# A two-layer retention and state-space decoder: the opening's norm ranked first, and the SSD norm's weight loaded earlier

## The chip, the cores and the metric

The kernel runs on one core of one Trainium2 chip. The metric is device time of one execution in microseconds (us); a kernel's time is the median over its runs. The engines are TensorE (PE), VectorE (DVE), ScalarE (ACT), GpSimd (POOL) and SyncE (SP), which only issues DMAs here. Each engine executes its instructions in the order of the program and waits on semaphores where an input isn't there yet.

## The reference

What is computed, cut to its frame (sequence 256, width 1024, two layers, float32):

```python
def hybrid_mixer(h, ...):                       # h is rmsnorm(x, norm_mix_w[l])
    u = h @ w_in
    q, k, v, g_ret, z, xbc, dt, gate_ret, gate_ssd = split(u)
    qf, kf = rotary(q, pos), rotary(k, pos) * RET_DK ** -0.5
    yr = retention(qf, kf, v)                   # 4 heads, decaying causal attention in chunks of 128
    yr = silu(g_ret) * (yr * rsqrt(mean(yr * yr) + EPS))
    o_ret = yr @ ret_out
    xs, bm, cm = split(silu(causal_dwconv(xbc, conv_w, conv_b)))
    ys = ssd_scan(xs * dtp, dtp * a, bm, cm) + d_skip * xs      # 32 heads in 4 groups
    ys = ys * silu(z)
    ys = ys * rsqrt(mean(ys * ys, per group) + EPS) * ssd_norm_w
    o_ssd = ys @ ssd_out
    return (sigmoid(gate_ret) * o_ret + sigmoid(gate_ssd) * o_ssd) @ w_o

for l in range(DEPTH):
    h = h + hybrid_mixer(rmsnorm(h, norm_mix_w[l]), ...)
    h = h + swiglu(rmsnorm(h, norm_ffn_w[l]), w_gate_up[l], w_down[l])
return rmsnorm(h, final_norm_w)
```

## The kernel before

All activations stay in SBUF; the weights, some 260 MB with what is read more than once, stream in from HBM. The 256 tokens are two halves of 128 (`t` is 0 or 1). Each float32 product is made of three float32r matmuls: a weight piece (`raw`, up to 128x1024 elements, 512 KB) arrives by DMA, ScalarE copies its high part (`wh`, L506), VectorE subtracts to get the low part (`wl`, L531), and TensorE multiplies high by high, low by high and high by low (L548, L549 and L550 with the weights stationary, L1034 and L1037 with the activations `xT` stationary). Some projections use a seven-product scheme on sums of weight blocks, which VectorE forms (L230) or a DMA issued by POOL adds up while it loads (L413).

**The order of the work** is set when the program is built, by a planner (`Flow`). Streams (Python generators) yield operations, each with an engine, an estimated cost, an emitting function and a priority `pr`; an engine of the planner's model takes the ready operation with the smallest `pr`, the older one on a tie. What each engine takes, in that order, is the program. The chip then follows that order, whatever its own durations are. Jobs (one projection each) have priorities from 0 up, in their order; the splitting of a job's weights stands a little ahead of the job. A `yield` on a slot semaphore such as `wbS` waits until a buffer is free.

**Weight loads** go through SyncE's queue (`feeder`, L486), in the order of the jobs, each as a `raw` slot comes free. Other loads are put in between: `BESIDE` (L206) gives for each entry of the list `others` (L2229) the number of the weight piece ahead of which it goes. The list holds the four quarters of x for the norm (`O`), constants, the opening norm's weight (the sixth entry), parameters, constants, and the starts of two tables (`tables(0)` is `load_angles`, `tables(1)` `load_decays`).

**The opening.** The first products (two heads of v, L874, `C` holding split x) are made from x before it is normed, twelve matmuls for each of eight k blocks; then comes the first job of the retention gate (`gr`, 48 matmuls of width 352, L548 to L550). Beside them the opening norm is worked out for each token half: ScalarE squares and sums x (`sil,ss<-O`), VectorE makes the mean (`ms`), POOL the power (`rstd`, L243), VectorE scales by `rstd` and the weight `wb` (`sil<-O,rstd,wb`, L233, two instructions of 512 columns), TensorE transposes (`tr<-cst,sil`, L644, eight of 128x128 for a half), ScalarE copies the high part into `xT`, VectorE subtracts the low part (`xT<-tr,xT`), and ScalarE keeps a plain copy (`plain`). `arrived` (L2185) starts this with the priority `PR0` (L205, 1.2). The jobs after gr use `xT`, the first with L1034.

**The buffer `wb`** (512 KB, one slot, `wbS`) holds by turns: the opening norm's weight, the rotary angles (`load_angles`, L1573, its DMA at L1580), the two halves of the SSD norm's weight (`ssd_w(0)`, `ssd_w(1)`), the FFN norm's weight, the next layer's norm weight. `load_wb` (L667) waits for the slot, issues a broadcast DMA (L672) from POOL, or from SyncE for the opening, and waits for its landing. The angles give up the slot after their last use in `rotary` (`turned` at 0, L1484). Both `ssd_w` streams are started when the job z begins in the plan (`z_begins`, L1892). Their loads are first used by z's norm (`sil<-sil,rz,wb`).

**The retention output stage** (layer 0 around 303 to 330 us, layer 1 around 922 to 948 us) multiplies the retention output by sums of the blocks of `ret_out` and `w_rw`: SyncE loads `raw<-in_w_rw_dram` and `raw<-in_ret_out_dram`, POOL issues accumulating loads `raw` and `dec<-in_w_rw_dram` (L413), ScalarE copies finished accumulators out of PSUM (`sx<-acc`, L223) between its weight copies, and TensorE's next group of matmuls into that accumulator (L548) waits for the copy. SyncE also loads `seg<-acs` there for the SSD scan.

Of the kernel before, what the change touches and what calls it, by code (L numbers as in the profile page):

```python
# [192 lines left out]
def trunk_kernel(  # L193
# [8 lines left out]
    SLOW, MT_SLACK = 1500.0, 800.0  # L202
    ADDS = 600.0
    ZS_PR, SAVE, DEC_AT = 1.0, 2000.0, 9000.0
    PR0, SLACK = 1.2, 2500.0  # L205
    BESIDE = (9, 11, 13, 15, 10, 14, 15, 15, 46, 44)  # L206
    APARTS, SUMS_PR = {}, 3.5
    cp = ctx.enter_context(tc.tile_pool(name="cp", bufs=1))
    wp = ctx.enter_context(tc.tile_pool(name="wp", bufs=HB))
# [7 lines left out]
    fl = Flow()  # L217
# [257 lines left out]
    def feeder(beside):  # L475

        for i, (src, k, n, job, (sem, alloc), land) in enumerate(specs):
            for at, gen in beside:
                if at == i:
                    yield from gen  # L480
            yield sem
            queue, eng, pr = (nc.sync, "sp", job) if i else (nc.scalar, "act", -4)

            def load():
                raw = alloc()
                queue.dma_start(out=raw[:, : k * n], in_=src)  # L486
                return raw

            raw = yield Op(eng, 450, load, pr)
            fl.spawn(land(raw, fl.transfer(512 * k * n, 4 * k * n)))  # L490
# [176 lines left out]
    def load_wb(src, pr, eng="pool"):  # L667
        yield wbS

        def emit():  # L670
            w = new_wb()
            (nc.sync if eng == "sp" else nc.gpsimd).dma_start(out=w, in_=src.partition_broadcast(P))  # L672
            return w

        w = yield Op(eng, 450 if eng == "sp" else 1050, emit, pr)
        yield fl.transfer(4 * P * D)
        return w
# [633 lines left out]
    def layer(l, mix, nxt, opening=None):  # L1311
# [261 lines left out]
        def load_angles():  # L1573
            if l:
                yield DEC_AT
            yield wbS

            def emit():
                w = new_wb()
                nc.sync.dma_start(out=w[:, : 2 * SEQ], in_=consts[:, K_COS:K_DEC])  # L1580
                return w[:, :SEQ], w[:, SEQ : 2 * SEQ]

            a = yield Op("sp", 450, emit, -1)
            fl.transfer(8 * P * SEQ)
            fl.set(angles, a)

        if l:
            fl.spawn(load_decays())
            fl.spawn(load_angles())
        else:  # L1590
            first_tables.extend([load_angles, load_decays])
# [271 lines left out]
        def ssd_w(i):  # L1863
            w = yield from load_wb(ssd_norm_w[l][i * D : (i + 1) * D], at_job[0])
            fl.set(wbs[i], w)
# [25 lines left out]

        def z_begins(g):  # L1892
            if g == 0:
                for i in range(2):
                    fl.spawn(ssd_w(i))
            if g == 2:
                fl.spawn(seven_sums(zops, yz, (0, 1), "A", at_job[0] + ZS_PR))

        def z_job(g):
            z_begins(g)  # L1900
            return tm_job(xT, z_post(g))
# [266 lines left out]
    def whole():  # L2168
# [62 lines left out]
        fl.spawn(opening.load(0))  # L2231
        fl.spawn(feeder([*zip((2, 6, 7), (opening.load(i) for i in range(1, 4))), *zip(BESIDE, others)]))
        for l in range(DEPTH):
            yield from layer(l, norms[l], norms[l + 1], None if l else opening)
# [87 lines left out]
```

## Time and profile before

| what | value |
|---|---|
| median of 3 runs | 1253.92 us (1253.69 to 1253.99) |
| the profiled execution's own time | 1253.99 us |
| its span in the profile | 1252.2 us |
| TensorE busy | 1238.6 us, 99% |
| VectorE, ScalarE, POOL busy | 1104.9 us (88%), 872.7 us (70%), 72.7 us (6%) |
| mean granted TensorE clock | 0.999 |
| bytes moved, mean rate | 266.07 MB, 212 GB/s |

How to read it: the span runs from the first to the last instruction of the trace; the execution's own time holds about 1.8 us more around it. In a timeline row stand the start, the duration, the engine, the line, the operation, the tile written and the tiles read, and in brackets how long the engine stood idle just before and what ended that. Matmuls overlap, so their durations are longer than their spacing; a loss on TensorE is read from the starts. `SPq` rows are DMA issues.

### The profile page before, as it was taken

What the parts mean: (1) busy time and instruction counts of PE and PEld (TensorE: products, weight loads), DVE (VectorE), ACT (ScalarE), POOL (GpSimd) and SP (SyncE); (2) the same over time, 40 slices, a digit from 0 to 9 for tenths busy, and PEclk for the clock granted to TensorE, in tenths of its full rate; (3) what the DMA queues carried; (4) which work ended last, traced back from release to release, by engine and by line L of the source; (5) the groups of instructions that cost most, each with busy time, mean ns of one, the idle gap of its engine ahead of it and who ended that gap; (6) DMA issues with size and microseconds to landing.
All of it is one profiled execution on the core that took longest, in us unless ns stands there. A gap on an engine that the chain in (4) does not pass through costs nothing.

```text
span 1252.2 us, 17656 instructions
## 1 busy us (share of the span) xinstructions
PE 1238.6 (99%) x6293; PEld 1052.0 (84%) x6293; DVE 1104.9 (88%) x1515; ACT 872.7 (70%) x1310; POOL 72.7 (6%) x92
## 2 busy tenths in 40 slices
PE   9999999999999999999999999999999999999997
PEld 7889888888788788888888898888888888888886
DVE  6998888889899978999798978879889998899995
ACT  7967776886766565786586676867957664776863
POOL 0000000001012001001000000000010110010000
PEclk9999999999999999999999999999999999999999
DMA  9658455566777757877776574554676776678871
GB/s 349 234 147 287 149 188 183 166 212 148 259 247 186 236 184 232 300 214 221 242 259 228 141 247 163 174 181 152 235 203 217 237 217 219 218 207 255 295 208 62
DMA packets 76343, 266.07 MB, mean 212 GB/s; under 512 B 8768, under 2 KB 9664, under 8 KB 76256
## 3 DMA queue, kind: packets, MB, share of 16 engines
q1 hardware_dynamic: 68272, 236.93, 54.2%
q0 software_dynamic: 7552, 27.38, 12.0%
q8 instruction: 49, 0.80, 0.3%
q10 hardware_dynamic: 432, 0.66, 0.2%
q14 instruction: 38, 0.31, 0.1%
HBM read 262.76 MB, written 2.16 MB: 212 GB/s over the span
## 4 chain that ended last, share of the span: by engine, by line
PE 69%; issue 2%; DVE 1%; DMA 1%; ACT 1%; POOLq 0%; POOL 0%; DVEq 0%; ACTq 0%
PE acc L548 15%; PE acc L550 15%; PE acc L549 15%; PE acc L1034 12%; PE acc L1037 6%; PE tr L644 2%; DMA raws<-in_w_sw_dram 1%; PE yps L1784 1%; DVE wl L531 1%; ACT wh L506 1%; DVE D L230 0%; PE ips L1771 0%; DVE sx L230 0%; PE tr L1671 0%; PE acc L1500 0%
## 5 line engine op out<-in xcount | busy, mean ns | idle before, releaser
L531 DVE TENSOR_TENSOR wl<-raw,wh 128x1024 fp32r<-128x1024 f32 (+2 forms) x387 | 457.1, 1197 | 42.2 <-ACT wh L506 41.0
L506 ACT ACTIVATE wh<-raw 128x1024 fp32r<-128x1024 f32 (+2 forms) x387 | 395.2, 1037 | 118.5 <-PE acc L550 49.7
L1034 PE MATMUL acc<-xT,wh 128*128 128x512 f32 x960 | 251.0, 395 | 1.0 <-DVE xT L230 1.0
L548 PE MATMUL acc<-wh,xT 128*128 128x512 f32 (+1 forms) x568 | 220.6, 388 | 0.0
L550 PE MATMUL acc<-wh,xT 128*128 128x512 f32 (+1 forms) x568 | 216.1, 380 | 0.0
L549 PE MATMUL acc<-wl,xT 128*128 128x512 f32 (+1 forms) x568 | 215.9, 380 | 0.0
L1034 PEld LDWEIGHTS acc<-xT,wh 128*128 128x128 f32 x960 | 170.3, 189 | 29.6 <-DVE xT L230 1.3
L1037 PEld LDWEIGHTS acc<-xT,wl 128*128 128x128 f32 x960 | 131.8, 190 | 9.9
L1037 PE MATMUL acc<-xT,wl 128*128 128x256 f32 x960 | 136.2, 283 | 0.0
L549 PEld LDWEIGHTS acc<-wl,xT 128*128 128x128 f32 x568 | 106.7, 188 | 20.8 <-issue 1.4
L548 PEld LDWEIGHTS acc<-wh,xT 128*128 128x128 f32 x568 | 106.7, 188 | 20.5 <-issue 1.4
L550 PEld LDWEIGHTS acc<-wh,xT 128*128 128x128 f32 x568 | 106.7, 188 | 19.6
L506 ACT ACTIVATE wh<-raws 128x1024 fp32r<-128x1024 f32 x80 | 83.9, 1057 | 46.9 <-DVE raws L230 16.5
L531 DVE TENSOR_TENSOR wl<-raws,wh 128x1024 fp32r<-128x1024 f32 x80 | 96.6, 1220 | 16.0 <-ACT wh L506 15.7
L548 PE MATMUL acc<-wh,A 128*128 128x512 f32 x224 | 88.6, 395 | 0.0
L550 PE MATMUL acc<-wh,A 128*128 128x512 f32 x224 | 87.6, 391 | 0.0
L549 PE MATMUL acc<-wl,A 128*128 128x512 f32 x224 | 87.2, 389 | 0.0
L233 DVE SCALAR_TENSOR_TENSOR cc<-cc,cv 128x255 f32<-128x255 f32 (+2 forms) x144 | 67.6, 478 | 11.4 <-ACT cc L223 10.3
L550 PEld LDWEIGHTS acc<-wh,A 128*128 128x128 f32 x224 | 42.0, 188 | 9.4 <-DVE A L230 0.5
L223 ACT ACTIVATE sx<-acc 128x512 f32<-128x512 f32 (+1 forms) x62 | 32.5, 525 | 25.0 <-PE acc L1034 14.2
L549 PEld LDWEIGHTS acc<-wl,A 128*128 128x128 f32 x224 | 42.1, 188 | 8.3
L548 PEld LDWEIGHTS acc<-wh,A 128*128 128x128 f32 x224 | 42.1, 188 | 8.4
(202 smaller groups left out, 1992.7 us busy)
## 6 DMA issues: line engine op xcount, KB each, us to landing
raw<-in_w_tm_dram SPq DMA_DIRECT2D x100, 512.0 KB, 4.1
raw<-in_w_fm_dram SPq DMA_DIRECT2D x80, 512.0 KB, 3.9
raw<-in_w_gf_dram SPq DMA_DIRECT2D x40, 512.0 KB, 4.4
raw<-in_w_gate_up_dram SPq DMA_DIRECT2D x32, 512.0 KB, 7.2
raw<-in_w_down_dram SPq DMA_DIRECT2D x28, 512.0 KB, 6.0
raw<-in_w_gr_dram SPq DMA_DIRECT2D x24, 352.0 KB, 4.3
seg<-acs SPq DMA_DIRECT2D x16, 512.0 KB, 5.9
raw<-in_ret_out_dram SPq DMA_DIRECT2D x16, 512.0 KB, 4.2
```

What stands on the lines that cost most here:

```text
L223: return Op("act", cost, lambda: nc.scalar.activation(out=out, in_=in_, func=func, **kw), pr, TABLES.get(func))
L233: return Op("dve", 1.04 * n + 130, lambda: nc.vector.scalar_tensor_tensor(out=out, in0=in0, scalar=scalar, in1=in1, op0=op0, op1=op1), pr)
L506: nc.scalar.activation(out=wh[:, :m], in_=raw[:, :m], func=AF.Copy)
L531: nc.vector.tensor_tensor(out=wl[:, :m], in0=raw[:, :m], in1=wh[:, :m].bitcast(F32), op=ALU.subtract)
L548: nc.tensor.matmul(ps, lhsT=lh, rhs=rh, start=first, stop=False, **kw)
L549: nc.tensor.matmul(ps, lhsT=lh, rhs=rl, start=False, stop=False, **kw)
L550: nc.tensor.matmul(ps, lhsT=ll, rhs=rh, start=False, stop=last, **kw)
L644: nc.tensor.transpose(out=ps[:, j * P : (j + 1) * P], in_=src[:, j * P : (j + 1) * P], identity=ident)
L1034: nc.tensor.matmul(box[0], lhsT=wh[:, k, fsl], rhs=x[:, k, :, :], start=(half, k) == (0, 0), stop=(half, k) == (1, 3))
L1037: nc.tensor.matmul(box[0][:, :SEQ], lhsT=wl[:, k, fsl], rhs=xh[:, k, :], start=False, stop=False)
L1784: nc.tensor.matmul(ps[:, i * HD : (i + 1) * HD], lhsT=sg[:, i, :], rhs=xdt[:, i * HD : (i + 1) * HD], start=True, stop=True)
```

## The change

Three edits. The opening norm's priority `PR0` goes from 1.2 to -0.5, below every job's. The opening norm's weight goes one place forward in SyncE's queue: ahead of weight piece 13 instead of 14. And `ssd_w(0)` is started right behind the load of the rotary angles, so that it stands next in line for the `wb` slot; `ssd_w(1)` is started at z as before. The third edit acts in both layers.

```diff
-    PR0, SLACK = 1.2, 2500.0
-    BESIDE = (9, 11, 13, 15, 10, 14, 15, 15, 46, 44)
+    PR0, SLACK = -0.5, 2500.0
+    BESIDE = (9, 11, 13, 15, 10, 13, 15, 15, 46, 44)
@@ load_angles
             a = yield Op("sp", 450, emit, -1)
             fl.transfer(8 * P * SEQ)
             fl.set(angles, a)
+            fl.spawn(ssd_w(0))
@@ z_begins
             if g == 0:
-                for i in range(2):
-                    fl.spawn(ssd_w(i))
+                fl.spawn(ssd_w(1))
```

Every engine has as many instructions of each kind as before. What moves: in the first 110 us the order on TensorE, VectorE, ScalarE and SyncE, and in both layers one DMA on POOL. Lines behind L1585 have numbers higher by one after the change (the seg load at L1737 is then at L1738).

On TensorE in the opening, the difference around the last two k blocks of L874 (`tr<-cst,sil` are the norm's transposes of token half 0, `wh` and `wl` the weight parts):

```order
 L874 MATMUL acc<-wl,C 128x512
 L874 MATMUL acc<-wh,C 128x512 x2
+L644 MATMUL tr<-cst,sil 128x128 x4
 L874 MATMUL acc<-wl,C 128x512
+L644 MATMUL tr<-cst,sil 128x128 x4
 L874 MATMUL acc<-wh,C 128x512 x2
 L874 MATMUL acc<-wl,C 128x512
```

Half 0's eight transposes, which stood behind the last L874, now stand on either side of the last L874 of the seventh k block, ahead of the twelve of the eighth. Half 1's eight, which stood ahead of the last three of gr's 48 matmuls, now stand ahead of the last eighteen.

On VectorE in the opening, before (from the mean of token half 0, `ms<-ss,ms`, to the first part of `xT` of half 1):

```order
20 L238 TENSOR_SCALAR ms<-ss,ms 128x1
21 L531 TENSOR_TENSOR wl<-raw,wh 128x704
22 L233 SCALAR_TENSOR_TENSOR sil<-O,rstd,wb 128x512 x2
23 L531 TENSOR_TENSOR wl<-raw,wh 128x704
24 L233 SCALAR_TENSOR_TENSOR Y<-acc,rstd,A 128x512 x2
25 L531 TENSOR_TENSOR wl<-raw,wh 128x1024
26 L230 TENSOR_TENSOR xT<-tr,xT 128x4x128 x2
27 L531 TENSOR_TENSOR wl<-raw,wh 128x1024 x2
28 L238 TENSOR_SCALAR ms<-ss 128x1
```

and after, the same stretch (`Y` is v with the norm's factor put in):

```order
20 L238 TENSOR_SCALAR ms<-ss,ms 128x1
21 L233 SCALAR_TENSOR_TENSOR sil<-O,rstd,wb 128x512 x2
22 L531 TENSOR_TENSOR wl<-raw,wh 128x704 x2
23 L230 TENSOR_TENSOR xT<-tr,xT 128x4x128 x2
24 L233 SCALAR_TENSOR_TENSOR Y<-acc,rstd,A 128x512
25 L531 TENSOR_TENSOR wl<-raw,wh 128x1024
26 L233 SCALAR_TENSOR_TENSOR Y<-acc,rstd,A 128x512
27 L238 TENSOR_SCALAR ms<-ss 128x1
28 L238 TENSOR_SCALAR ms<-ss,ms 128x1
```

Half 0's scaling by `wb` stands ahead of a weight subtraction that it stood behind, `xT` ahead of `Y`, and half 1's mean ahead of two weight subtractions. Further on, half 1's `xT` has a weight subtraction between it and its `Y`, where the two `dtt` stood.

On POOL, the difference in layer 0 (`rr` are powers for the retention norm, `raw` and `dec<-in_w_rw_dram` the accumulating loads of the retention output stage; the numbers behind `rr` are buffers):

```order
 L243 TENSOR_TENSOR rr_1849<-ms,mhalf 128x2
 L243 TENSOR_TENSOR rr_2095<-ms,mhalf 128x2
-L243 TENSOR_TENSOR rr_2325<-ms,mhalf 128x2
+L672 DMA wb<-in_ssd_norm_w_dram 128x1024
+L243 TENSOR_TENSOR rr_2327<-ms,mhalf 128x2
 L413 DMA raw<-in_w_rw_dram 128x1024 x2
 L413 DMA dec<-in_w_rw_dram 128x1024 x2
-L672 DMA wb<-in_ssd_norm_w_dram 128x1024
 L243 TENSOR_TENSOR rz<-ms,mhalf 128x1 x4
 L672 DMA wb<-in_ssd_norm_w_dram 128x1024
```

The first half of the SSD norm's weight moves from behind the four accumulating loads to a place ahead of the fourth `rr`, where POOL's queue waits until the rotary angles have left the slot. Layer 1 shows the same. On SyncE, the opening norm's weight (`wb<-in_norm_mix_w_dram`, L672) moves from behind the third piece of `in_w_gr_dram` to ahead of it, and the load `acs<-side` (L1447) behind two pieces of `in_w_tm_dram` that it stood ahead of.

## The prediction

> **What bounds the kernel now.** I read the share of busy time first, then the list of TensorE's waits, then the timeline around each wait that the change can touch. In the page, first row and clock row:
>
> ```profile
> PE 1238.6 (99%) x6293; PEld 1052.0 (84%) x6293; DVE 1104.9 (88%) x1515; ACT 872.7 (70%) x1310; POOL 72.7 (6%) x92
> ...
> PEclk9999999999999999999999999999999999999999
> ```
>
> TensorE is busy 1238.6 of the span's 1252.2 us, at full clock in every slice. It does the same work after the change, so only its 13.6 us of idle time can be won. The list of its waits (us in total, times, longest):
>
> ```profile
> PE acc L548 <- ACT sx L223: 3.7, 5, 0.9
> PE acc L1034 <- DVE xT L230: 1.0, 1, 1.0
> ...
> PE tr L644 <- DVE sil L233: 0.3, 1, 0.3
> ```
>
> The last two stand in the opening, four of the first five in the retention output stage, two in each layer. The change touches both places.
>
> **Part 1: the opening norm ranked first.** TensorE's timeline (start us, duration us):
>
> ```profile
> 24.97 0.39 PE L874 MATMUL acc<-wl,C 128*128 128x512 f32 x1
> ...
> 27.93 1.03 PE L644 MATMUL tr<-cst,sil 128*128 128x128 f32 x8
> 28.72 0.41 PE L548 MATMUL acc<-wh,C 128*128 128x352 f32 x1
> ...
> 35.84 0.32 PE L550 MATMUL acc<-wh,C 128*128 128x352 f32 x1
> 36.41 1.29 PE L644 MATMUL tr<-cst,sil 128*128 128x128 f32 x8 [0.25 <-DVE sil L233]
> 37.46 0.41 PE L548 MATMUL acc<-wh,C 128*128 128x352 f32 x1
> 37.71 0.33 PE L549 MATMUL acc<-wl,C 128*128 128x352 f32 x1
> 37.87 0.32 PE L550 MATMUL acc<-wh,C 128*128 128x352 f32 x1
> 39.22 1.20 PE L1034 MATMUL acc<-xT,wh 128*128 128x512 f32 x4 [1.02 <-DVE xT L230]
> ```
>
> Starts tell the loss, since matmuls overlap. Undisturbed, a 352-wide matmul follows after 0.16 us (37.71 to 37.87) and eight transposes take 0.79 (27.93 to 28.72). Token half 1's transposes start 0.57 after the matmul before (0.41 lost) and last 1.05 (0.26 lost: the second four wait for the second half of sil); L1034 starts 1.35 after its predecessor (1.19 lost). Sum 1.86 us. Why they are late, on VectorE, and the two SyncE rows that matter:
>
> ```profile
> 25.30 1.41 DVE L233 SCALAR_TENSOR_TENSOR sil<-O,rstd,wb 128x512 f32<-128x512 f32 x2 [0.59 <-DMA wb<-in_norm_mix_w_dram]
> ...
> 35.51 1.42 DVE L233 SCALAR_TENSOR_TENSOR sil<-O,rstd,wb 128x512 f32<-128x512 f32 x2 [0.67 <-POOL rstd L243]
> ...
> 38.16 0.40 DVE L233 SCALAR_TENSOR_TENSOR dtt<-acc,rstd,prm 128x32 f32<-128x32 f32 x2
> 16.93 0.42 SPq L2178 DMA_DIRECT2D O<-in_x_dram  x1
> ...
> 18.46 0.42 SPq L672 DMA_DIRECT2D wb<-in_norm_mix_w_dram  x1
> 20.00:30.00 10.00, 10.00 (x52) 8.58 (x51) 8.18 (x13) 7.09 (x12) 0.55 (x1) 1.00 1.03 377
> 30.00:40.00 10.00, 8.69 (x53) 7.81 (x52) 9.03 (x16) 10.00 (x20) 0.55 (x1) 1.00 0.72 234
> ```
>
> (The last two are the table of windows: stretch, its length, busy us of PE, PEld, DVE, ACT and POOL, clock, DMA share, GB/s.) The DMA engines are full from 20 to 30 us, at 377 GB/s. The norm weight wb passes one 352 KB piece (360,448 bytes), so it lands 360,448 / 377e3 = 0.96 us sooner at most; I take 0.9, so 24.3 instead of 25.2 (sil started at 25.30 on its landing). The two sils follow at 24.4 and 25.1. The first four transposes of token half 0 now stand ahead of the L874 that started at 24.97, and with it ahead of the twelve L874 of the last k. They need sil's end (24.4 + 0.70 = 25.1) and a hop of 0.2 to TensorE: 25.3. That is a new wait of 0.35 us, on TensorE in order, with those twelve queued behind it; before, half 0's transposes waited for nothing. The second four need 0.7 more, and TensorE spends that on four transposes (0.4) and one L874 (0.23): 0.1 lost.
>
> Half 1's transposes stand 18 matmuls (18 x 0.16 = 2.9 us) ahead of L1034 instead of 3 (0.5), 2.4 us more cover. VectorE in turn gets one weight subtraction (1.20 by the row below) ahead of xT's low part, and loses the two dtt (0.40). L1034's wait: 1.19 - 2.4 + 1.2 - 0.4, below zero by 0.4, so it goes. The 0.26 inside the eight transposes stays, since two sils still follow each other; ahead of them I leave 0.1, since squares, rstd and sil come ahead of ScalarE's and VectorE's weight work. New loss 0.35 + 0.1 + 0.1 + 0.26 = 0.8; gain 1.86 - 0.8, about 1.0 us. Bounds: wb a full 0.96 us earlier, 1.1; wb not earlier at all (first wait 1.25), 0.15.
>
> ```profile
> L531 DVE TENSOR_TENSOR wl<-raw,wh 128x1024 fp32r<-128x1024 f32 (+2 forms) x387 | 457.1, 1197 | 42.2 <-ACT wh L506 41.0
> ```
>
> The later shuffles of weight work up to 110 us I cost at nothing: TensorE lists no wait there. What hides them is the other engines' lead, and ScalarE has none between 30 and 40 us (10.00 of 10). If it gives way, up to half the opening's gain returns as small waits.
>
> **Part 2: the ssd norm's weight leaves the retention output stage.** The first half of that weight is 512 KB, issued by POOL; the next rows are layer 0's POOL row, ScalarE, TensorE, and the DMA issues of 304 to 325 us (KB each, median us to landing) with two windows:
>
> ```profile
> 305.49 0.89 POOL L672 DMA_DIRECT2D wb<-in_ssd_norm_w_dram  x1
> 316.08 1.06 ACT L506 ACTIVATE wh<-raw 128x1024 fp32r<-128x1024 f32 x1 [3.00 <-DMA raw<-in_w_rw_dram]
> 320.02 0.50 PE L548 MATMUL acc<-wh,O 128*128 128x512 f32 x1 [0.81 <-ACT sx L223]
> ...
> 326.67 0.50 PE L548 MATMUL acc<-wh,Y 128*128 128x512 f32 x1 [0.91 <-ACT sx L223]
> wb<-in_ssd_norm_w_dram POOLq DMA_DIRECT2D x1, 512.0 KB, 10.3
> ...
> raw<-in_w_rw_dram SPq DMA_DIRECT2D x1, 512.0 KB, 10.0
> 312.00:316.00 4.00, 4.00 (x27) 3.64 (x26) 2.30 (x3) 1.06 (x1) 0.00 (x0) 1.00 1.02 396
> 316.00:320.00 4.00, 3.21 (x14) 2.27 (x13) 2.42 (x3) 3.92 (x11) 0.00 (x0) 1.00 1.03 419
> ```
>
> ScalarE stood 3.00 us for one weight piece, in the order of its queue, and the copy sx that frees TensorE's accumulator stands behind. From 316 to 320 it is busy 3.92 of 4.00: it never recovers its lead, so both TensorE waits hang on that landing. wb and the awaited piece take about 10 us each and end together (wb at 305.49 + 10.3 = 315.8, the piece where ScalarE starts, at 316.08), in a stretch where the DMA engines are full. Without wb there are 524,288 bytes fewer ahead of the piece: 1.25 us at 419 GB/s, 1.32 at 396; I take 1.28. ScalarE's chain moves forward by that much: the first wait (0.81) goes, the second shrinks by the rest. Limit: 0.81 + 0.91 = 1.72. So 1.28 in layer 0.
>
> The Trainium skill ("DMA: Bandwidth & Descriptors", Anatomy of one DMA) gives a transfer's variable part as bytes over 436 GB/s, an estimate of 1.20 us here: the sum below would be 3.4 instead of 3.6. The windows above show 396 to 419, so the measurement decides.
>
> Layer 1, the same stage:
>
> ```profile
> 934.89 1.06 ACT L506 ACTIVATE wh<-raw 128x1024 fp32r<-128x1024 f32 x1 [2.74 <-DMA raw<-in_w_rw_dram]
> 938.83 0.50 PE L548 MATMUL acc<-wh,O 128*128 128x512 f32 x1 [0.55 <-ACT sx L223]
> ...
> 945.48 0.50 PE L548 MATMUL acc<-wh,Y 128*128 128x512 f32 x1 [0.92 <-ACT sx L223]
> ```
>
> 0.55 + 0.92 = 1.47 is the limit, again above 1.28.
>
> **Part 3: the new place of that weight.** It now waits for the angles' last use and goes out on POOL behind the third rr; wb's first use (z, the last row) is far later, so its landing is not on the path:
>
> ```profile
> 200.60 0.69 DVE L230 TENSOR_TENSOR cc<-cc,wb 128x512 f32<-128x512 f32 x1
> 220.84 0.69 POOL L243 TENSOR_TENSOR rr<-ms,mhalf 128x2 f32<-128x2 f32 x1 [25.38 <-DVE ms L238]
> 200.00:210.00 10.00, 10.00 (x50) 8.16 (x49) 9.30 (x16) 4.72 (x7) 0.00 (x0) 1.00 0.55 161
> 206.53 1.06 ACT L506 ACTIVATE wh<-raw 128x1024 fp32r<-128x1024 f32 x1 [3.00 <-PE acc L550]
> L233 DVE SCALAR_TENSOR_TENSOR sil<-sil,rz,wb x16: 741/748/752, 349.0 to 1008.9; 128x512 f32<-128x512 f32 x16
> ```
>
> The angles come free at 201.3 (200.60 + 0.69). What is queued behind the waiting issue on POOL is the fourth rr at 220.84, which POOL reached 25.38 us early: no cost. The DMA engines are 0.55 busy there, and ScalarE waits on TensorE, not on a load, so an extra 1.25 us of transfer fits: cost 0, at most 1.25 us of delay on the loads and, since ScalarE has 3 us to spare, hardly any of it on TensorE. The Trainium skill (same page, Queues, rings and completion order) says that each DMA engine takes packets from its queue rows by turns, so the loads behind would be held back for the 512 KB, not longer; no run here shows it yet at this place.
>
> **How the numbers follow.** Sum: 1.0 + 1.28 + 1.28 = 3.6 us, from the profiled run's own 1253.99 (span 1252.2 and 1.8 around it; 0.07 above the median of the runs): **1250.4 us**. A measurement of this kernel can tell about 0.2%, 2.5 us, from no change; faster means under 1251.4. Chances:
>
> **Forecast as summed**, 0.58: own range 1249.6 to 1251.8 (opening 0.15 to 1.1, layers 1.0 to 1.7 each); about 0.50 of it counts as faster.
>
> **More is freed** (0.07): if ScalarE's lead grows by more than 1.28, since the accumulating loads on POOL's queue land sooner too, both layers give 1.72 + 1.47: 1.1 + 3.2 = 4.3, 1249.7; with the slow restart after each wait (0.50 against 0.39) 1249.2.
>
> **The opening gives nothing** (0.13): ScalarE is full and VectorE at 9.03 of 10 from 30 to 40 us, so the lead taken by the norm is missing from weights. Against it: DMA share is 0.72 there and TensorE idles 1.31. Only the layers remain: 1253.99 - 2.56 = 1251.4, on the bound; half counts as faster.
>
> **The layers give nothing** (0.15): the change doesn't do there what it moves bytes for. The awaited piece could be held by its own queue (the seg transfer ahead of it on SyncE) or the accumulating transfers, and not by wb. For: 10.0 us is long for 512 KB. Against: engines full, and wb and piece landing together. Time: 1253.99 - 1.0 = 1253.0.
>
> **Slower** (0.04): TensorE, in order, holds the last twelve L874 behind a transpose that waits for wb. In the trace before, wb took 6.8 us here (issued at 18.46, sil at 25.30). Each us beyond 24.0 of landing is a us of wait; the opening loses from 25.4 on, the whole kernel from 27.9, by over 0.2% from 30.4. With the 10.3 us of layer 0, from an issue anywhere between 17.4 (behind the x row at 16.93) and 18.5: 27.7 to 28.8, a wait of 3.7 to 4.8, total 1253.7 to 1254.8. Against: fewer bytes stand ahead of it than before.
>
> The remaining 0.03 are mixtures near 1252. Faster 0.50 + 0.07 + 0.07 = 0.64 and a little of the mixtures: 0.65; slower 0.04; same 0.31. The range, 1249.2 to 1253.1, takes in all but the slower case and the edges of the others.
>
> **What would show it.** Right: TensorE's transposes at about 25.3 with a wait of 0.3 to 0.4; L1034's wait on xT gone; ScalarE's 3.00 and 2.74 us waits for the w_rw piece down to about 1.7 and 1.5; L548's waits at 320 and 939 gone and the second ones near 0.5 to 0.8 and 0.2 to 0.5; no new TensorE wait at 205 to 215 or 820 to 835. Wrong: the piece's issue to landing still near 10 us (Part 2), a transpose wait above 1 us, or new waits between 40 and 110 us (Part 1).

## The result, and the profile after

The changed kernel takes 1249.63 us (median of 6 runs, 1248.81 to 1250.66), the kernel before 1253.75 us (median of 6, 1253.11 to 1253.99). The ratio of the runs is 0.9966, with a 95% interval of 0.9955 to 0.9976: 4.1 us faster, where 3.6 were forecast. The profiled execution took 1250.49 us, its span 1248.7 us, against 1253.99 and 1252.2 before.

The list of TensorE's waits after the change (us in total, times, longest):

```profile
PE idle L2198 <- DVE mhalf L2175: 1.3, 1, 1.3
PE acc L548 <- ACT sx L223: 0.8, 3, 0.4
PE acc L1423 <- DVE side L238: 0.7, 1, 0.7
PE tr L644 <- DVE D L230: 0.7, 2, 0.3
PE tr L644 <- DVE sil L233: 0.6, 1, 0.6
```

L548's waits fell from 3.7 to 0.8 us and L1034's wait for `xT` is gone. Two entries are longer or new: the transposes' wait for sil (0.6 instead of 0.3), and a wait of L1423 that the list before does not hold. TensorE's timeline in the opening and at that new wait:

```profile
25.21 0.66 PE L644 MATMUL tr<-cst,sil 128*128 128x128 f32 x4 [0.59 <-DVE sil L233]
...
38.24 1.08 PE L1034 MATMUL acc<-xT,wh 128*128 128x512 f32 x4
...
83.17 0.41 PE L1423 MATMUL acc<-pol,side 128*128 128x32 f32 x2 [0.70 <-DVE side L238]
```

and VectorE's rows that answer to them:

```profile
24.41 1.42 DVE L233 SCALAR_TENSOR_TENSOR sil<-O,rstd,wb 128x512 f32<-128x512 f32 x2 [1.29 <-DMA wb<-in_norm_mix_w_dram]
...
82.87 0.24 DVE L238 TENSOR_SCALAR side<-cst 128x128 f32<-128x128 f32 x1
```

The weight let sil start at 24.41 (forecast 24.4), the transposes started at 25.21 (25.3), the first L1034 at 38.24 instead of 39.22. By 83 us TensorE waited for a small tile, `side`, that VectorE now makes behind a weight subtraction. Before, TensorE reached L1423 at 81.53 without a wait; it is later now by its order too, since 221 matmuls instead of 212 stand between the first L1034 and L1423.

The wait at 83 us can be followed backwards through the traces. VectorE's second subtraction of a 1024-wide weight piece now stands behind half 1's mean and sil, 4.1 us later. It frees a `raw` slot, so SyncE sends its next two pieces 4.1 and 5.5 us later (first two rows before, the others after):

```profile
31.91 2.35 DVE L531 TENSOR_TENSOR wl<-raw,wh 128x1024 fp32r<-128x1024 f32 x2
33.16 1.46 SPq L486 DMA_DIRECT2D raw<-in_w_fm_dram  x2
...
35.98 1.22 DVE L531 TENSOR_TENSOR wl<-raw,wh 128x1024 fp32r<-128x1024 f32 x1
37.27 2.82 SPq L486 DMA_DIRECT2D raw<-in_w_fm_dram  x2
```

The `in_w_tm_dram` pieces behind them start going out when they did before (41.01 us, before 40.95), now right after those two, and take longer to land: a median of 6.2 us over the window from 30 to 48 us, instead of 4.0. That the two groups of loads crowd each other is read from these rows; no run tests it. ScalarE then waits for two of these pieces, where before it waited for no load, and VectorE waits for the copy `cc`, which stands behind them in ScalarE's order:

```profile
45.74 1.06 ACT L506 ACTIVATE wh<-raw 128x1024 fp32r<-128x1024 f32 x1 [1.51 <-DMA raw<-in_w_tm_dram]
48.70 1.06 ACT L506 ACTIVATE wh<-raw 128x1024 fp32r<-128x1024 f32 x1 [1.90 <-DMA raw<-in_w_tm_dram]
...
50.06 0.42 DVE L230 TENSOR_TENSOR cc<-acc,cc 128x256 f32<-128x256 f32 x1 [1.15 <-ACT cc L223]
```

From there to `side` at 82.87 VectorE stands idle for only 0.3 us, so the 1.15 us are still missing when TensorE asks for that tile.

In the retention output stages, ScalarE's row for the awaited w_rw piece (layer 0, layer 1):

```profile
314.18 1.06 ACT L506 ACTIVATE wh<-raw 128x1024 fp32r<-128x1024 f32 x1 [1.35 <-DVE wl L531]
...
931.00 1.06 ACT L506 ACTIVATE wh<-raw 128x1024 fp32r<-128x1024 f32 x1 [1.22 <-DMA raw<-in_w_rw_dram]
```

TensorE there:

```profile
324.76 0.50 PE L548 MATMUL acc<-wh,Y 128*128 128x512 f32 x1 [0.37 <-ACT sx L223]
...
941.58 0.50 PE L548 MATMUL acc<-wh,Y 128*128 128x512 f32 x1 [0.24 <-ACT sx L223]
```

and the DMA issues of 304 to 325 us (KB each, median us to landing):

```profile
dec<-in_w_rw_dram POOLq DMA_DIRECT2D x1, 512.0 KB, 8.3
raw<-in_w_rw_dram SPq DMA_DIRECT2D x1, 512.0 KB, 8.4
```

ScalarE's waits of 3.00 and 2.74 us are 1.35 and 1.22, the first L548 wait of each layer is gone, the second is 0.37 and 0.24 instead of 0.91 and 0.92. The piece lands 8.4 us after its issue instead of 10.0. (In the first row the profile names VectorE; the piece's landing at about 305.72 + 8.4 = 314.1, SyncE's issue being at 305.72, is what came last.)

At the weight's new place, POOL's row:

```profile
201.38 0.60 POOL L672 DMA_DIRECT2D wb<-in_ssd_norm_w_dram  x1 [6.13 <-DVE cc L230]
```

It goes out at 201.38 (201.3 was forecast), lands 5.0 us later, and no TensorE wait stands between 84 and 320 us.

Where the 3.5 us between the two profiled spans come from, by TensorE's starts: at the first L1771 at 207 us, which is past the opening and the wait at 83, the gain is 0.21 us (207.02 to 206.81). The stretch of the layer 0 output stage (from the first L1771 of the layer's third pair to that of its fourth) shrinks from 48.59 to 46.93 us, 1.66; that of layer 1 from 48.34 to 46.83, 1.51. The rest, 0.1, are small shifts elsewhere of both signs. So in this one execution the layers gave 3.2, and the opening almost nothing.

### The profile page after: what moved, and what is told of

Same layout as the page of the kernel before. It is cut to its first block, busy times and chain, and to the rows that moved or that the text cites. A ratio compares the mean times of both kernels' runs of the same rounds, so it can differ in the third digit from the quotient of the medians.

```text
span 1248.7 us, 17651 instructions
## 1 busy us (share of the span) xinstructions
PE 1237.9 (99%) x6293; PEld 1051.8 (84%) x6293; DVE 1105.3 (89%) x1515; ACT 871.8 (70%) x1310; POOL 72.8 (6%) x92
## 4 chain that ended last, share of the span: by engine, by line
PE 92%; DMA 3%; DVE 2%; issue 1%; ACT 1%; SPq 0%; POOLq 0%; POOL 0%; ACTq 0%; DVEq 0%
PE acc L548 19%; PE acc L550 19%; PE acc L549 19%; PE acc L1034 18%; PE acc L1037 9%; PE tr L644 2%; PE yps L1785 2%; DMA raws<-in_w_sw_dram 1%; DVE wl L531 1%; DMA raw<-in_w_v_dram 1%; DMA wb<-in_norm_mix_w_dram 1%; PE tr L1672 1%; PE acc L1500 1%; PE ips L1772 1%; ACT wh L506 0%
## 5 line engine op out<-in xcount | busy, mean ns | idle before, releaser
L1034 PE MATMUL acc<-xT,wh 128*128 128x512 f32 x960 | 250.9, 395 | 0.0
L548 PE MATMUL acc<-wh,xT 128*128 128x512 f32 (+1 forms) x568 | 220.5, 388 | 0.0
L1034 PEld LDWEIGHTS acc<-xT,wh 128*128 128x128 f32 x960 | 170.5, 189 | 28.3 <-issue 0.2
L548 PEld LDWEIGHTS acc<-wh,xT 128*128 128x128 f32 x568 | 106.7, 188 | 20.6 <-issue 1.4
L548 PE MATMUL acc<-wh,A 128*128 128x512 f32 x224 | 88.5, 395 | 0.0
L548 PEld LDWEIGHTS acc<-wh,A 128*128 128x128 f32 x224 | 42.1, 188 | 8.2
```

The costliest lines, as they stand in the source:

```text
L548: nc.tensor.matmul(ps, lhsT=lh, rhs=rh, start=first, stop=False, **kw)
L1034: nc.tensor.matmul(box[0], lhsT=wh[:, k, fsl], rhs=x[:, k, :, :], start=(half, k) == (0, 0), stop=(half, k) == (1, 3))
```

## The experiments

The theory to test, A: the opening's gain is real, but the order behind it gives part back at 83 us; and the layers' gain is the 512 KB taken from in front of the awaited w_rw piece. Rivals are told with each run. Each kernel ran beside its own runs of the kernel before, and a gain is taken by the ratio to them. Their median was 1254.12 us for the first four kernels below, 1253.26 for the weight on SyncE inside the stretch, the norm's weight one more piece forward and the changed kernel again, and 1253.57 for the other four. "Stage wait" below is ScalarE's idle time ahead of the copy of that piece, in layer 0 and layer 1; before it was 3.00 and 2.74.

**The third edit alone** (PR0 1.2 and the sixth entry of BESIDE 14, the rest as changed).

> The third edit alone: the first half of the SSD norm's weight loaded behind the angles, the opening as before. Theory A (the 512 KB collide with the awaited w_rw piece in both retention output stages; the trace after the change has that piece landing about 1.5 to 1.65 us sooner there): about 3.2 us faster than before, 1250.5, ScalarE's 3.00 and 2.74 us waits down to about 1.3, the first L548 wait of each layer gone, no wait of L1423 at 83 us. Rival B (the gain comes from the opening, the layers only follow): within 0.5 us of before, both L548 waits of a layer still there.

Measured 1251.26 us, ratio 0.9976 (0.9967 to 0.9985): 3.0 us faster. ScalarE's two rows, and L1034 in the opening:

```profile
315.00 1.06 ACT L506 ACTIVATE wh<-raw 128x1024 fp32r<-128x1024 f32 x1 [1.42 <-DMA raw<-in_w_rw_dram]
...
931.99 1.06 ACT L506 ACTIVATE wh<-raw 128x1024 fp32r<-128x1024 f32 x1 [1.28 <-DVE wl L531]
```

```profile
39.14 1.19 PE L1034 MATMUL acc<-xT,wh 128*128 128x512 f32 x4 [1.02 <-DVE xT L230]
```

The opening is that of before, with its 1.02 us wait, and the layers have their whole gain (stretches 47.00 and 46.87). Rival B is out.

**The first two edits alone** (`ssd_w` as before).

> The first two edits alone: the norm ranked first and its weight one place forward, the SSD norm's weight as before. Theory A: the first L1034 about 1.0 us earlier in the opening against the first L874, but a wait of 0.7 us of L1423 on VectorE's side tile at 83 us gives nearly all of it back: 0 to 0.4 us faster than before, 1253.5; ScalarE's waits for the w_rw piece still near 3 us. Rival B: 3 to 4 us faster than before. Rival D (the wait at 83 us is chance of one execution and not of the order): no such wait, 1.0 us faster, 1252.7.

Measured 1252.97 us, ratio 0.9991 (0.9982 to 1.0000): about 1.1 us faster, the interval just reaching no change. Together with the run above that is 4.1, the whole effect. In its trace:

```profile
38.91 1.08 PE L1034 MATMUL acc<-xT,wh 128*128 128x512 f32 x4
...
83.15 0.41 PE L1423 MATMUL acc<-pol,side 128*128 128x32 f32 x2
```

```profile
315.98 1.06 ACT L506 ACTIVATE wh<-raw 128x1024 fp32r<-128x1024 f32 x1 [3.04 <-DMA raw<-in_w_rw_dram]
```

The layers are as before. In the opening theory A missed: the wait of 0.7 us is not there, although the order is that of the changed kernel on TensorE, VectorE and ScalarE. TensorE was itself later (38.91), and VectorE had waited less for `cc` (0.46 us instead of 1.15), so that the two meet at 83.15. The time lies nearer to rival D.

**The first edit alone** (PR0 -0.5, the weight's place as before).

> The first edit alone: the norm ranked first, its weight where it was in SyncE's queue. Theory A: the first transposes wait for the weight about 0.9 us longer than with the second edit (about 1.5 instead of 0.6 us, if the order keeps them ahead of the last k block), so that the first L1034 comes 0.1 us earlier than before instead of 1.0; total 0 to 0.8 us slower than before with the wait at 83 us, 1253.7 to 1254.5. Rival E (the second edit does nothing, the rank is all): the same first L1034 as with both edits.

Measured 1253.43 us, ratio 0.9991 (0.9982 to 1.0000), the same ratio as with both. The planner, which reckons with the weight's later landing, put the first transposes four matmuls further back than in the changed kernel:

```profile
26.80 0.66 PE L644 MATMUL tr<-cst,sil 128*128 128x128 f32 x4 [0.45 <-DVE sil L233]
...
35.26 0.63 PE L644 MATMUL tr<-cst,sil 128*128 128x128 f32 x4 [0.44 <-DVE sil L233]
...
39.05 1.09 PE L1034 MATMUL acc<-xT,wh 128*128 128x512 f32 x4
```

The first L1034 is 0.17 us earlier than before, as A said, and not 0.98. The order behind it differs too, and no wait at 83 us follows; the total does not tell the two apart.

**The changed kernel with the `side` tile made earlier in layer 0.**

```diff
-            yield 4000.0
+            yield 4000.0 if l else 3000.0
             yield silS
...
+            if not l:
+                yield 2000.0
             yield accS
```

> The changed kernel with VectorE's side tile of layer 0 made one weight subtraction earlier, TensorE's order kept (the planner's delay ahead of that tile 3000 instead of 4000 in layer 0, and 2000 behind it). Theory A (that one misplaced subtraction is what gives the opening's gain back): the 0.7 us wait of L1423 at 83 us goes and 0.7 to 0.9 us of it reach the end, 1248.8. Rival F (VectorE is late there as a whole, the wait comes back at the next thing that it makes): within 0.3 us of the changed kernel, 1249.6, with a new wait on VectorE between 83 and 110 us.

Measured 1249.66 us, ratio 0.9964 (0.9952 to 0.9977), the changed kernel's own time. The wait of L1423 is gone; 7 us later stands a smaller one, on VectorE again:

```profile
88.70 0.43 PE L549 MATMUL acc<-wl,xT 128*128 128x352 f32 x1 [0.17 <-DVE wl L531]
```

Rival F fits better: not one misplaced instruction, but VectorE late as a whole. In this trace too it had waited for `cc` near 50 us, for 1.12 us. The gain of 0.7 to 0.9 us is not to be seen in the time.

**The weight issued by SyncE, so late that it falls behind the busy stretch** (first two edits, `ssd_w(0)` at z as before with `eng="sp"`; TensorE's, VectorE's and ScalarE's orders are those of the first two edits alone).

> The first two edits, and the first half of the SSD norm's weight started at z as before, but issued by SyncE, where it falls behind five w_tm pieces and so behind the busy stretch; the order on TensorE, VectorE and ScalarE is that of the first two edits alone. Theory A (what counts is that these 512 KB are not in front of the awaited w_rw piece; where else they go doesn't matter): the piece lands 8.2 to 8.4 us after its issue instead of 9.8 to 10.0, ScalarE's waits 1.3 instead of 3.0 and 2.6, 1.5 us less in each layer, time as after the change, 1249.7. Rival C (the gain came from the early place at the angles, or from z's norm no longer waiting): 1253.

Measured 1248.92 us, ratio 0.9962 (0.9948 to 0.9975). The weight went out at 328.53 instead of 305.49; the stage waits:

```profile
313.34 1.06 ACT L506 ACTIVATE wh<-raw 128x1024 fp32r<-128x1024 f32 x1 [1.32 <-DVE wl L531]
...
929.99 1.06 ACT L506 ACTIVATE wh<-raw 128x1024 fp32r<-128x1024 f32 x1 [1.11 <-DMA raw<-in_w_rw_dram]
```

The piece lands 8.3 us after its issue. Late is as good as early; what counts is that the 512 KB are out of the stretch. Rival C is out.

**Half of it left in place**: 256 KB by POOL at z, 256 KB by SyncE behind the stretch.

> The first two edits, and the first half of the SSD norm's weight in two DMAs: 256 KB by POOL at z as before, the other 256 KB by SyncE behind the busy stretch. Theory A (the price is the bytes): half of it, ScalarE's wait for the w_rw piece about 2.2 us in layer 0 and 1.9 in layer 1, each layer 0.7 to 0.8 us faster than with the whole transfer. Rival G (the price is that POOL's queue row has work beside SyncE's at all, while it takes every second turn): the wait stays at 2.8 or more.

```profile
313.62 1.06 ACT L506 ACTIVATE wh<-raw 128x1024 fp32r<-128x1024 f32 x1 [2.40 <-DMA raw<-in_w_rw_dram]
...
931.20 1.06 ACT L506 ACTIVATE wh<-raw 128x1024 fp32r<-128x1024 f32 x1 [1.77 <-DMA raw<-in_w_rw_dram]
```

2.40 and 1.77, beside 2.2 and 1.9 expected: the price goes roughly with the bytes, and rival G in the form that the mere presence of work on POOL's queue costs all of it is out. (One run, 1250.45 us.)

**The same bytes on SyncE's queue, ahead of the seg load.**

> The first two edits, and the same 512 KB issued by SyncE just ahead of the seg load, so in the same stretch and ahead of the awaited w_rw piece, but not on POOL's queue; the order on TensorE, VectorE and ScalarE is that of the first two edits alone. Theory A (bytes ahead of the piece, on whichever queue): ScalarE's wait near 3.0 and 2.6 us again, both L548 waits there. Rival G (1.28 us is the price of the bytes, the 0.2 to 0.4 us measured above it come from sharing between POOL's and SyncE's queues): wait 2.6 and 2.3 us.

It did not test that. SyncE is held up at the seg load, and what stands ahead of it goes out long before:

```profile
293.77 0.33 SPq L486 DMA_DIRECT2D raw<-in_w_rw_dram  x1
294.15 0.49 SPq L1747 DMA_DIRECT2D wb<-in_ssd_norm_w_dram  x1
```

So the stage wait was 1.66 in layer 0 and 1.16 in layer 1, close to that without the bytes (one run, 1248.54 us). The expectation was also wrong on the order: behind the stretch the plan had changed. ScalarE's table load and exp of seg (1.28 and 1.06 us) moved from ahead of the copy `sx` to behind it, and that took the second L548 wait away by itself. The next three kernels have this moved exp too. They are therefore compared with the kernels above by the stage wait, which lies ahead of that point; their totals hold the exp's share as well.

**The same bytes on SyncE's queue, inside the stretch** (behind the seg load, ahead of the piece).

> The earlier try with SyncE put the weight ahead of the seg load, and it left 11 us before the stretch, because the queue was only held up behind it. Here the same 512 KB are issued by SyncE right behind that seg load and ahead of the awaited w_rw piece, so inside the stretch; else the first two edits alone. Theory A (bytes ahead of the piece, on whichever queue): ScalarE's wait for the piece 2.6 to 3.0 us in layer 0 and 2.3 to 2.6 in layer 1, both L548 waits of each layer back. Rival G (the bytes cost only on POOL's queue, by turns with SyncE's): at most 1.7 us, as without them.

```profile
315.37 1.06 ACT L506 ACTIVATE wh<-raw 128x1024 fp32r<-128x1024 f32 x1 [2.58 <-DMA raw<-in_w_rw_dram]
...
932.14 1.06 ACT L506 ACTIVATE wh<-raw 128x1024 fp32r<-128x1024 f32 x1 [2.25 <-DMA raw<-in_w_rw_dram]
```

2.58 and 2.25, nearer to theory A. Over the five traces without these bytes in the stretch (both of the changed kernel, the third edit alone, the earlier side tile, SyncE behind the stretch) the stage waits average 1.38 and 1.17; over the three with all of them on POOL's queue (before, and the first two edits together and the first alone) 3.06 and 2.63. On POOL's queue the 512 KB cost 1.68 and 1.46, on SyncE's 1.20 and 1.08. (Against the kernel ahead of the seg load, whose order is the same on TensorE, VectorE and ScalarE, SyncE's are 0.92 and 1.09.) TensorE's stretches agree for POOL's queue: over the same three and five traces they average 48.65 against 46.97 in layer 0 and 48.22 against 46.77 in layer 1, so 1.68 and 1.45 reach TensorE. Neither theory had this whole: the bytes cost on either queue, and in this one execution on SyncE's they cost about 0.4 us less than on POOL's. Why is open; the runs don't tell whether it is the turns that two queues take or the broadcast load's own pace there. (One run, 1250.23 us.)

**The seg load behind the last w_rw piece**, on top of the earlier side tile: `yield 800.0` ahead of the seg DMA of the last group's first chunk.

> The changed kernel with the earlier side tile of layer 0 and, in both layers, the seg load of the last group's first chunk issued behind the last w_rw piece instead of ahead of it; no other engine's order changes against the side tile alone. Theory A (the piece is still late by what stands ahead of it): the piece lands about 1.2 us sooner, ScalarE's remaining wait of 1.35 us goes, and with it the second L548 wait of each layer (0.54 and 0.34 by the starts): 0.6 to 0.9 us faster than with the side tile alone, 1248.2 to 1249.0. Rival H (ScalarE's chain is then held by the seg tile itself, which lands later): the wait moves to the seg activations, 1249.6.

Measured 1248.93 us, ratio 0.9960 (0.9946 to 0.9973). The piece lands 7.6 us after its issue, the stage waits are down to ScalarE's pace, and TensorE's list holds no wait of L548 on sx; a wait on VectorE takes part of it back:

```profile
312.58 1.06 ACT L506 ACTIVATE wh<-raw 128x1024 fp32r<-128x1024 f32 x1 [0.25 <-PE acc L550]
...
928.94 1.06 ACT L506 ACTIVATE wh<-raw 128x1024 fp32r<-128x1024 f32 x1 [0.24 <-PE acc L550]
```

```profile
PE acc L550 <- DVE A L230: 1.1, 2, 0.5
```

0.7 us below the side tile alone by the medians, as expected, but 0.5 by the ratios, and well inside the two intervals; and the moved exp has a share in it, so that theory A and the new order can't be told apart here. The expectation's sentence that no other engine's order changes was wrong.

**The opening norm's weight one more piece forward**, on top of that (the sixth entry of BESIDE 12).

> The version with the earlier side tile and the seg load behind the w_rw piece, and the opening norm's weight one more piece forward in SyncE's queue (12 instead of 13). Theory A (the first transposes wait for this weight, 0.6 to 0.9 us in three of the traces): it lands about 1 us sooner, no wait above 0.3 us there, 0.3 to 0.7 us faster than the version without, 1248.4. Rival I (other things end last at the transposes, rstd or the x rows, which the weight now pushes back): same time, 1248.9.

Measured 1248.33 us (5 runs, 1247.66 to 1249.22), ratio 0.9959 (0.9947 to 0.9972). The planner now sets all eight transposes of half 0 ahead of the last ten L874, and they wait for nothing:

```profile
25.70 1.03 PE L644 MATMUL tr<-cst,sil 128*128 128x128 f32 x8
...
90.08 0.43 PE L549 MATMUL acc<-wl,xT 128*128 128x352 f32 x1 [0.48 <-DVE wl L531]
```

But the first L1034 is at 38.13, no earlier than in the changed kernel, the wait on VectorE stands at 90 us, and at 207.09 the first L1771 is no earlier than before the change. The time is 0.6 us below the version without by the medians and 0.1 by the ratios, so rival I's same time can't be told from theory A's gain. The weight is then not the bound of the opening; in most executions of the changed kernel's order it wasn't either, as the part on the prediction shows.

**The changed kernel again**, beside the same runs of before as the version above.

> The changed kernel itself once more, on the same chip and beside the same runs of before as the version above. If the wait at 83 us belongs to single executions (it stood in two traces of five with that order), this trace has its first L1034 anywhere from 37.5 to 38.9 and the wait anywhere from 0 to 0.9 us; the time 1249.6 again. If it belongs to the order, the wait is 0.5 us or more.

Measured 1249.94 us (7 runs, 1248.51 to 1250.65), ratio 0.9971 (0.9960 to 0.9982).

```profile
38.11 1.08 PE L1034 MATMUL acc<-xT,wh 128*128 128x512 f32 x4
...
82.71 0.41 PE L1423 MATMUL acc<-pol,side 128*128 128x32 f32 x2 [0.37 <-DVE side L238]
```

The version above is 1.6 us below it on the same chip, with ranges that overlap (1247.66 to 1249.22, and 1248.51 to 1250.65): it beats the kernel before clearly, the changed kernel probably.

The opening over the executions of both orders, from the rows of TensorE and VectorE (the kernels with the `side` tile moved and the first edit alone are left out, since their order differs):

| trace | first L1034 | VectorE's wait for `cc` near 50 us | L1423's wait | first L1771 | L1034 to L1771 |
|---|---|---|---|---|---|
| before | 39.22 | none | none | 207.02 | 167.80 |
| third edit alone | 39.14 | none | none | 206.95 | 167.81 |
| changed | 38.24 | 1.15 | 0.70 | 206.81 | 168.57 |
| first two edits | 38.91 | 0.46 | none | 206.79 | 167.88 |
| SyncE behind the stretch | 38.12 | 0.63 | none | 206.00 | 167.88 |
| half in place | 37.50 | none | none | 205.16 | 167.66 |
| SyncE ahead of seg | 37.69 | 1.16 | 0.52 | 206.08 | 168.39 |
| SyncE in the stretch | 38.05 | 1.48 | 0.85 | 206.76 | 168.71 |
| changed, again | 38.11 | 0.87 | 0.37 | 206.36 | 168.25 |

The seven with the new order have their first L1034 at 38.09 on average, 1.09 earlier than the two of before; at 207 us they are at 206.28, 0.70 earlier. So the opening's gain is real, 0.4 us of it is lost by 207 us, and one execution differs from the next by more than that (37.50 to 38.91). The last column says where the loss is: it is longer by 0.4 to 0.9 us in the four executions with L1423's wait, and by at most 0.1 in the three without. That wait appears where VectorE stood for 0.87 us or more near 50 us and not where it stood for 0.63 or less. So it goes with VectorE's wait for `cc`, and this in turn with the two loads that ScalarE waits for: 3.30 to 3.78 us together in the four, 2.42 to 2.93 in the three.

## Why the prediction was right, point by point

- **The first transposes.** Weight landing, sil and transposes came within 0.1 us of the working in the profiled execution; the new wait was 0.59 by the profile where 0.35 was worked out. But of the seven executions with that order only two wait there, the first of the changed kernel and that of the first two edits alone (0.89). In these, sil waited for the weight and TensorE's first L874 had started at 5.49 and 5.52. In the other five it started at 6.03 or 6.04, as in the trace before, sil waited for `rstd` from POOL instead and started at 23.87 to 24.05, and the transposes waited for nothing. The weight had landed by then: 5.9 us after an issue at 17.10 to 17.30, so at about 23.1, 2 us sooner than before. The working's limit of 0.96 us did not hold there, and that its wait appears in the first profiled execution is partly luck.
- **L1034's wait** went, in every execution with the new order. The term of 1.0 us holds at that place: 0.98 in the profiled execution, 1.09 on average over seven.
- **"The later shuffles of weight work up to 110 us I cost at nothing".** This is the step that failed, by 0.4 us on average. The prediction named the price, up to half of the opening's gain back as small waits, and the engine, ScalarE without lead between 30 and 40 us; the sum then left it out because TensorE listed no wait there before. ScalarE's lead did run out, at 45 to 49 us, when it waited for two weight pieces, and the loss came to TensorE through VectorE at 83 us. It is 0.37 to 0.85 us in four of seven executions and absent in the three where those pieces kept ScalarE for less than 3 us. The prediction's own sign for this, new waits between 40 and 110 us, appeared. With `side` made earlier, the next thing that VectorE makes was late in two of three executions, by 0.17 and 0.48.
- **The layers, 1.28 each.** The mechanism was right (third edit alone, half the bytes, the bytes late): the collision, not the place at the angles. The size was low: the stretches shrank by 1.66 and 1.51 in the profiled execution, and the stage wait fell by 1.68 and 1.46 on average. 1.28 was the price of the bytes at the full rate, and on SyncE's queue, in one execution, they cost 1.20 and 1.08; on POOL's, beside SyncE's, about 0.4 more. The case "more is freed", with its limits of 1.72 and 1.47, came nearer than the main one, but not for its reason: the last accumulating load landed 8.2 us after its issue before and 8.3 after the change in layer 0, and 8.3 both times in layer 1. So why POOL's bytes cost more than their time at the full rate stays open.
- **The new place of the weight** cost nothing, as worked out.
- That the sum agrees is partly luck, because two misses work against each other: the opening gave about 0.3 less, the layers 0.6 more. The rival that the layers give nothing is refuted by the third edit alone. That the opening gives nothing is refuted at 38 us, and nearly held at 207 us in the one execution that was profiled first. Its mechanism, lead taken by the norm and missing from the weights, is what the rows from 32 to 50 us show, at a part of its price.

## What to carry to other kernels

A transfer that nobody waits for can still set the pace: look at what shares the DMA engines with the piece that somebody does wait for, and move the idle one to either side of the full stretch. What a static order wins at one place is worth only what the engines behind have in lead; follow it to a mark well behind the change before counting it. A wait of some tenths in one trace needs a second execution before it is called a property of the order, and it is worth following back to where it began, here from a matmul at 83 us to a weight load sent at 37.

## What the runs showed of the hardware

- A 512 KB load ahead of an awaited one, with the DMA engines full (share 1.02 and 1.03 from 312 to 320 us before), lengthened ScalarE's wait for it by 1.68 and 1.46 us from POOL's queue and by 1.20 and 1.08 from SyncE's; half the bytes on POOL's queue by 1.02 and 0.60 (one execution each for the last two).
- The Trainium skill ("DMA: Bandwidth & Descriptors", Anatomy of one DMA) has, for a DMA that GpSimd issues, bytes over 436 GB/s as the part that grows with size, an estimate of 1.20 us for these. The delay by SyncE's load comes near that figure, the delay by POOL's is longer.
- With the same order on TensorE up to 38 us, the first L1034 started between 37.50 and 38.91 us in seven executions, while the stretch of each output stage repeated to about 0.2 us (46.91 to 47.06 in layer 0 and 46.69 to 46.87 in layer 1 over five traces). So the start is the part that varies; the runs don't show why.
